# The output weights' four subtractions in the first pass of a decoder layer: from GpSimd to VectorE, in two pairs

## The chip, the cores and the metric

One core of a Trainium2 chip runs the kernel. The metric is the device time of one execution in microseconds (us). Engines are named as the profile does: PE is TensorE's matmul, PEld its weight load, DVE VectorE, ACT ScalarE, POOL GpSimd, SP SyncE, whose queue issues all the DMAs that the text speaks of.

## The reference, cut to what matters

One layer over 1024 positions of width 2048 in float32: one wide input projection, three mixers on its parts, an output projection, a residual and a layer norm.

```python
proj = jnp.einsum('bsd,de->bse', x, w_in[l])
...
y_att = forgetting_attention(...) * jax.nn.silu(g_att)
y_conv = short_conv_mixer(...) * jax.nn.silu(g_conv)
y_pool = multiscale_pool_mixer(...) * jax.nn.silu(g_pool)
y = jnp.concatenate([y_att, y_conv, y_pool], axis=-1)
y = jnp.einsum('bse,ed->bsd', y, w_out[l])
x = layer_norm(DEEPNORM_ALPHA * x + y, ln_g[l], ln_b[l])
```

Both projections are done by a fast block scheme (Strassen's, in a form with sums that share terms): each 2 x 2 block product takes seven products of blocks, and the blocks that go into them are sums and differences of the blocks of `x` and of the weights. For `w_out` these are the differences b22 - b12, b12 - b11, b22 - (b12 - b11) and b21 - (b22 - (b12 - b11)). Here the first pass makes them on the side and stores them in DRAM (`o_dram`), for the last stage of the kernel to load.

## The kernel before

**Products.** A float32 value goes into TensorE as two parts, high and low. `split` (L120) makes them: `L121` copies the source, rounded, on ScalarE (`hi`), and `L122` subtracts that from the source on VectorE (`lo`). `mm3` (L127) then runs three matmuls, `L128` high x high, `L129` high x low of `x`, `L130` low x high. So every operand of TensorE takes one `L121` and one `L122`, and the third matmul of a product is the first to need the result of `L122`. `operand` (L320) allocates both parts with the tag `h1`, name `wop`, in four buffers, which is two operands: the one in use and the next.

**The first pass** (`first_pass`, L529) goes over 28 pairs of weight columns, each a 2 x 2 of blocks of 128 x 1024. A pair's place in `order` is called turn n. Pairs 0 to 11 have turns of three products (steps `s2`, `s1`, `s3`), with the product `11` done before; pairs 12 to 27 have turns of four (`11`, `s2`, `s1`, `s3`). Up to turn 23 the two kinds alternate, three on even n, four on odd n; the last four turns are all of four. One product is 24 matmuls of 128x512, into a bank `aux` or `acc`. After `s2` VectorE adds the bank to `ca` (`L296`, to `u`); after `s1` it makes `cb` (`L304`); after `s3`, `ca` and `cb` (`L307`, `L308`), which are stored (`L309`, `L310`).

**What goes on beside a product** is written in `beside(p, name)` (L459), called after each. In the program's order: the next turn's pair is mixed (`Pair.mix`, L255, and `mix_last`, L268) at `s2` of a three-product turn or at `11` of a four-product one; the pair after that is loaded at `s1` (`load_place`, L252: blocks 0, 1, 3, 2, 512 KB each, tag `w1`, nine buffers, name `wb`). For the pairs of three products the mix is `L259` and `L260` on VectorE and `L261` on GpSimd; for those of four it is `L264` on GpSimd (`t`), and then `L265` and `L266` on VectorE. Each ends with `L270` on GpSimd, whose result is stored by `L273`. The scheduler draws mixes ahead of their written place: turn 11's, written at turn 10's `s2`, stands behind `L304` of turn 9 on VectorE.

**The output weights** are the class `OutBlocks` (L381). Sixteen of its blocks are done in turns 7 to 24, without 14 and 18 (`out_places`, L526). In such a turn n:

- at `s2`, `outs[n - 1].store()` (four stores of 256 KB, `L405`) and then `outs[n].load()` (four loads of 256 KB, `L392`, tiles `wo` of 128x512; three with the tag `wr`, which has four buffers, one with `wh`, which has three);
- at `s1`, `outs[n].mix()`: a fifth tile and four subtractions on GpSimd, `L397` to `L400`.

**What sets the order.** Each engine runs its instructions in one order, fixed when the program is built. A scheduler makes it out of the program's order and may move what is not held; `tc.keep_in_program_order` holds an instruction in its written place on its engine, as the stores and loads of `OutBlocks` are. The engines wait for each other by semaphores. The SP queue, too, is one order: a store in it that waits for its data holds every DMA behind it.

Of the kernel before, what the change touches and what calls it, by code (L numbers as in the profile page):

```python
# [36 lines left out]
ALU = mybir.AluOpType  # L37
# [36 lines left out]
def layer(ctx: ExitStack, tc: tile.TileContext, xt, x, wp, wf, b_f, conv_w, pool_w, pool_scale,  # L74
          w_out, ln_g, ln_b, out):
    nc = tc.nc
# [27 lines left out]
    def f4(name, tag):  # L104
        return tile_of([P, S], F32, name, tag)
# [5 lines left out]
    def half(name, tag):  # L111
        return tile_of([P, H], F32, name, tag)
# [128 lines left out]
    class Pair:  # L241
# [13 lines left out]
        def mix(self):  # L255
            r = self.raw
            if self.p < AHEAD:
                self.t1, self.t2, self.t3 = r[0], f4("t2", "w1"), r[1]
                nc.vector.tensor_tensor(self.t1, r[1], r[0], ALU.subtract)  # L259
                nc.vector.tensor_tensor(self.t2, r[3], self.t1, ALU.subtract)  # L260
                nc.gpsimd.tensor_tensor(self.t3, r[3], r[1], ALU.subtract)  # L261
            else:
                self.t1, self.t2, self.t3 = r[1], r[3], f4("t3", "w1")
                nc.gpsimd.tensor_tensor(self.t3, r[3], r[1], ALU.subtract)  # L264
                nc.vector.tensor_tensor(self.t1, r[1], r[0], ALU.subtract)  # L265
                nc.vector.tensor_tensor(self.t2, r[3], self.t1, ALU.subtract)  # L266

        def mix_last(self):  # L268
            r = self.raw
            nc.gpsimd.tensor_tensor(r[2], r[2], self.t2, ALU.subtract)  # L270
# [76 lines left out]
    def gate_sums(name, k0):  # L347

        acc = bank("aux")[: 2 * NH]
        for k in range(KH):  # L350
            w = fw[:, k0 + k].rearrange("p a b -> p (a b)")
            x = xs[name, k]
            nc.tensor.matmul(acc, w, x[:, 0], start=k == 0, stop=False)
            nc.tensor.matmul(acc, w, x[:, 1], start=False, stop=k == KH - 1)
        flat = half("gs", "wh")[: 2 * NH]
        nc.scalar.copy(flat, acc)
        return flat

    def turned_sums(flat):

        turned = bank("aux")[:, : 8 * NH].rearrange("p (a b) -> p a b", a=4)
        for st in range(4):
            nc.tensor.transpose(turned[:, st], flat[:, st * P : st * P + P], ident[: 2 * NH, : 2 * NH])
        return turned
# [3 lines left out]
    def load_s4(k):  # L368
        r21, r22, r11, r12 = (half("xr", "wr") for _ in range(4))
        for r, e, h in ((r21, k, 1), (r22, KH + k, 1), (r11, k, 0), (r12, KH + k, 0)):  # L370
            tc.keep_in_program_order(nc.sync.dma_start(r, xt[e, :, h * H : h * H + H]))
        s4_parts[k] = r21, r22, r11, r12

    def make_s4(k):
        r21, r22, r11, r12 = s4_parts.pop(k)
        nc.vector.tensor_tensor(r21, r21, r22, ALU.add)
        nc.vector.tensor_tensor(r21, r21, r11, ALU.subtract)
        nc.vector.tensor_tensor(r12, r12, r21, ALU.subtract)
        nc.sync.dma_start(s4_dram[k], r12)

    class OutBlocks:  # L381
# [5 lines left out]
        def load(self):  # L387
            i, k = self.i, self.k
            self.t = [half("wo", tag) for tag in ("wr", "wr", "wr", "wh")]
            for t, e, c in zip(self.t, (KH + k, KH + k, k, k), (0, 1, 0, 1)):  # L390
                src = w_out[e, :, i * S + c * H : i * S + c * H + H]
                tc.keep_in_program_order(nc.sync.dma_start(t, src))  # L392

        def mix(self):
            b11, b12, b21, b22 = self.t
            t3 = half("wo", "wh")
            nc.gpsimd.tensor_tensor(t3, b22, b12, ALU.subtract)  # L397
            nc.gpsimd.tensor_tensor(b12, b12, b11, ALU.subtract)
            nc.gpsimd.tensor_tensor(b22, b22, b12, ALU.subtract)
            nc.gpsimd.tensor_tensor(b21, b21, b22, ALU.subtract)  # L400
            self.t = b12, b22, t3, b21

        def store(self):
            for j, t in enumerate(self.t):
                tc.keep_in_program_order(nc.sync.dma_start(o_dram[self.i, j, self.k], t))  # L405
# [21 lines left out]
    def replace(name, tag, src):  # L427
        for k in range(KH):
            t = take(name, k, tag)
            r = half("xr", "wr")  # L430
            nc.sync.dma_start(r, src[k])
            split_tile(t, r)
# [30 lines left out]
    def load_place(n):  # L463
        order[n].load(0, 1, 3, 2)

    def beside(p, name):

        if name == "11" and p < AHEAD:
            if p == EARLY:
                load_place(0)  # L470
            if p == AHEAD - 2:
                load_place(1)
            if p == AHEAD - 1:
                order[0].mix()
                order[0].mix_last()
            return
        n = place[p]
        if name == ("s2" if p < AHEAD else "11") and n + 1 < N_PAIRS:
            order[n + 1].mix()
            order[n + 1].mix_last()  # L480
        if name == "s2" and n < N_PAIRS - 2:
            pairs[p].store_mixed()
            if n - 1 in outs:
                outs[n - 1].store()
            if n in outs:
                outs[n].load()
        if name in ("s2", "s3") and 3 <= n < 8:
            for k in s4_parts.copy():
                make_s4(k)
            if n < 7:  # L490
                load_s4(2 * n - 6 + (name == "s3"))
        if name == "s1":
            if n in outs:
                outs[n].mix()
            if n + 2 < N_PAIRS:
                load_place(n + 2)
            if n in gate_sums_at:
                env["sums"] = gate_sums(gate_sums_at[n], 0)
        if name == "s3":
            if n == 2:  # L500
                nc.vector.tensor_copy(fgt[:, :4], turned_sums(env["sums"]))
            if n == 3:
                nc.vector.tensor_tensor(fgt[:, 4:], fgt[:, :4], turned_sums(env["sums"]), ALU.subtract)
        if (n, name) == (N_PAIRS - 1, "11"):
            replace("12", "xa", xt[KH:, :, :H])
        if (n, name) == (N_PAIRS - 1, "s2"):
            for q in order[-2:]:
                q.store_mixed()
            replace("22", "xb", xt[KH:, :, H:])
        if (n, name) == (N_PAIRS - 1, "s1"):  # L510
            replace("s4", "xc", s4_dram)
            for q in (0, 1):
                t = half("c11", "wr")
                nc.sync.dma_start(t, a_dram[q, :, :H])
                banks_set.append(preset(t))

    def preset(block):

        acc = bank("acc")
        nc.scalar.copy(acc, block)  # L520
        return acc
# [4 lines left out]
    outs = {n: OutBlocks(m % 2, m // 2) for m, n in enumerate(out_places)}  # L526

    def first_pass():
        ahead_of = in_order()  # L529
        step = next(ahead_of)  # L530
        parts = operand(step[1]())
        while step:
            after_it = next(ahead_of, None)
            parts_after = None
            p, _, name, bank_of, follow = step
            if after_it and (p.p, name) != (AHEAD - 1, "11"):
                parts_after = operand(after_it[1]())
            multiply(parts, name, bank_of())
            follow()
            beside(p.p, name)  # L540
            if after_it and parts_after is None:
                parts_after = operand(after_it[1]())
            step, parts = after_it, parts_after
# [8 lines left out]
    def gate_logits(n):  # L552
# [12 lines left out]
    fgz, az, lf, before, t2, poly = (  # L565
        gate_tmp[:, i * NST * NH : (i + 1) * NST * NH].rearrange("p (a b) -> p a b", b=NH) for i in range(6))
# [244 lines left out]
    def pool_steps(g, u, gate):  # L811
# [43 lines left out]
        for slot, step in ((7, means), (9, split_pw), (13, split_z(0)), (14, split_z(1)), (16, mix(0)), (17, mix(1))):  # L855
            at(slot, step)
# [412 lines left out]
```

## Time and profile before

| | |
|---|---|
| time, median of 3 runs (lowest to highest) | 1660.64 us (1660.34 to 1664.97) |
| profiled execution: its own time, its span | 1661.48 us, 1659.4 us |
| PE busy in the span | 1561.2 us, 94% |
| DVE busy | 1116.7 us, 67% |
| ACT busy | 701.0 us, 42% |
| POOL busy | 517.4 us, 31% |
| DMA, mean | 205 GB/s |

The span is the profiled execution from its first to its last instruction; the execution's own time is longer by what lies around it. A busy share is a mean over the whole span, in which stages with different limits follow each other. Line numbers (L122) are those of the kernel before. A timeline's row gives the start, the duration, engine, line, operation and tile (out<-in), and in brackets how long the engine was idle before it and what ended that. A waits row gives the total idle time, the number of times and the longest.

### The profile page before, as it was taken

To read this page: it belongs to the slowest core of one execution; us is meant where nothing else is said; L and a number is where in the kernel's file an instruction comes from. 1 tells how busy PE (TensorE), PEld (TensorE's weight loads), DVE (VectorE), ACT (ScalarE), POOL (GpSimd) and SP (SyncE) were. 2 spreads that over 40 slices of the span, in tenths; PEclk is the share of its full clock that TensorE was granted. 3 is DMA by queue.
4 is the path that set the end of the run, shared out by engine and by line. 5 is a ranking of instruction groups with operands and counts; after the bars stand their busy time and mean duration, and the time that the engine had idled before them with its cause. 6 is when DMAs were issued, how large, how long until landed. Compare 5 with 4: busy or idle time off the path is not lost. (4 is left out here: it accounts for less than half of the span.)

```text
span 1659.4 us, 20213 instructions
## 1 busy us (share of the span) xinstructions
PE 1561.2 (94%) x6836; PEld 1258.9 (76%) x6836; DVE 1116.7 (67%) x1587; ACT 701.0 (42%) x1254; POOL 517.4 (31%) x381
## 2 busy tenths in 40 slices
PE   7999999999999989999999999989988999999985
PEld 6887777787787878788878777867766777788765
DVE  6754665676464556368686868677778884567777
ACT  4421211121111115457565657565666554434431
POOL 0132234666555541004141413343326231100005
PEclk9999999999999999999999999999999999999998
DMA  8755877887777775735545445445444446557552
GB/s 249 253 208 205 313 270 277 286 299 252 268 254 264 255 278 178 256 129 165 183 163 180 159 169 168 154 139 193 135 149 156 146 141 231 181 184 228 183 193 101
DMA packets 156807, 339.92 MB, mean 205 GB/s; under 512 B 17952, under 2 KB 27040, under 8 KB 156704
## 3 DMA queue, kind: packets, MB, share of 16 engines
q1 hardware_dynamic: 156704, 338.64, 60.2%
q8 instruction: 53, 0.87, 0.2%
q14 instruction: 50, 0.41, 0.1%
HBM read 247.28 MB, written 91.29 MB: 204 GB/s over the span
## 5 line engine op out<-in xcount | busy, mean ns | idle before, releaser
L122 DVE TENSOR_TENSOR wh<-wr,wh 128x512 fp32r<-128x512 f32 x272 | 203.2, 753 | 94.7 <-ACT wh L121 94.1
L121 ACT CAST wop<-wb 128x1024 fp32r<-128x1024 f32 x76 | 80.0, 1053 | 341.4 <-PE aux L129 173.1
L121 ACT CAST wh<-wr 128x512 fp32r<-128x512 f32 x272 | 166.4, 618 | 92.4 <-PE acc L130 27.8
L130 PE MATMUL aux<-xs,wop 128*128 128x512 f32 x448 | 178.4, 398 | 18.7 <-DVE wop L122 18.6
L130 PE MATMUL acc<-x,wh 128*128 128x512 f32 x448 | 177.6, 396 | 2.4 <-DVE wh L122 2.3
L128 PE MATMUL acc<-x,wh 128*128 128x512 f32 x448 | 178.4, 398 | 1.4 <-ACT wh L121 1.4
L128 PE MATMUL aux<-xs,wop 128*128 128x512 f32 x448 | 177.1, 395 | 0.0
L129 PE MATMUL aux<-xs,wop 128*128 128x512 f32 x448 | 176.6, 394 | 0.0
L129 PE MATMUL acc<-x,wh 128*128 128x512 f32 x448 | 176.2, 393 | 0.0
L122 DVE TENSOR_TENSOR wop<-wb,wop 128x1024 fp32r<-128x1024 f32 x76 | 120.6, 1587 | 41.6 <-ACT wop L121 41.5
L130 PEld LDWEIGHTS aux<-xs,wop 128*128 128x128 f32 x448 | 85.5, 191 | 42.2 <-DVE wop L122 23.9
L130 PEld LDWEIGHTS acc<-x,wh 128*128 128x128 f32 x448 | 84.6, 189 | 27.4 <-DVE wh L122 9.5
L128 PEld LDWEIGHTS acc<-x,wh 128*128 128x128 f32 x448 | 85.0, 190 | 20.5 <-ACT wh L121 5.1
L129 PEld LDWEIGHTS aux<-xs,wop 128*128 128x128 f32 x448 | 85.5, 191 | 18.3
L128 PEld LDWEIGHTS aux<-xs,wop 128*128 128x128 f32 x448 | 85.7, 191 | 17.8
L129 PEld LDWEIGHTS acc<-x,wh 128*128 128x128 f32 x448 | 85.1, 190 | 15.7
L130 PE MATMUL acc<-xs,wh 128*128 128x512 f32 x224 | 87.8, 392 | 3.4 <-DVE wh L122 3.4
L130 PE MATMUL acc<-xs,wop 128*128 128x512 f32 x224 | 87.7, 392 | 2.3 <-DVE wop L122 2.1
L704 POOL TENSOR_TENSOR m<-m,t 128x256 f32<-128x256 f32 (+1 forms) x64 | 69.9, 1092 | 63.2 <-ACT t L757 61.0
L128 PE MATMUL acc<-xs,wh 128*128 128x512 f32 x224 | 88.2, 394 | 0.0
L122 DVE TENSOR_TENSOR pt<-t,pt 128x512 fp32r<-128x512 f32 (+1 forms) x96 | 84.0, 888 | 6.3 <-ACT pt L121 6.1
L129 PE MATMUL acc<-xs,wh 128*128 128x512 f32 x224 | 87.4, 390 | 0.0
(269 smaller groups left out, 3733.1 us busy)
## 6 DMA issues: line engine op xcount, KB each, us to landing
wb<-wp SPq DMA_DIRECT2D x116, 512.0 KB, 5.7
wr<-wp SPq DMA_DIRECT2D x112, 256.0 KB, 2.8
wo<-w_out SPq DMA_DIRECT2D x64, 256.0 KB, 6.0
o_dram<-wo SPq DMA_DIRECT2D x64, 256.0 KB, 3.6
wr<-o_dram SPq DMA_DIRECT2D x64, 256.0 KB, 2.8
t_dram<-wb SPq DMA_DIRECT2D x28, 512.0 KB, 6.2
a_dram<-ca SPq DMA_DIRECT2D x28, 512.0 KB, 4.7
b_dram<-cb SPq DMA_DIRECT2D x28, 512.0 KB, 5.5
```

What stands on the lines that cost most here:

```text
L121: nc.scalar.copy(hi, src)
L122: nc.vector.tensor_tensor(lo, src, hi.bitcast(F32), ALU.subtract)
L128: nc.tensor.matmul(acc, wh, xh, start=start, stop=False, **more)
L129: nc.tensor.matmul(acc, wh, xl, start=False, stop=False, **more)
L130: nc.tensor.matmul(acc, wl, xh, start=False, stop=stop, **more)
L704: eng.tensor_tensor(kept[n][:, c0:], prev[:, c0:], t[n, j][:, c0:], op)
```

## The change

The four subtractions of `OutBlocks.mix` run on VectorE instead of GpSimd, through a helper (L395) that holds them in their written place. `mix`, at `s1`, keeps the first two. The last two move to a new `mix_last`, called at `s3`, after the third or fourth product of the turn. The lines behind move down: the stores from `L405` to `L411`. The arithmetic is the same.

```diff
--- before.py
+++ after.py
@@ -391,14 +391,20 @@
                 src = w_out[e, :, i * S + c * H : i * S + c * H + H]
                 tc.keep_in_program_order(nc.sync.dma_start(t, src))
 
+        def subtract(self, out, a, b):
+            tc.keep_in_program_order(nc.vector.tensor_tensor(out, a, b, ALU.subtract))
+
         def mix(self):
             b11, b12, b21, b22 = self.t
             t3 = half("wo", "wh")
-            nc.gpsimd.tensor_tensor(t3, b22, b12, ALU.subtract)
-            nc.gpsimd.tensor_tensor(b12, b12, b11, ALU.subtract)
-            nc.gpsimd.tensor_tensor(b22, b22, b12, ALU.subtract)
-            nc.gpsimd.tensor_tensor(b21, b21, b22, ALU.subtract)
+            self.subtract(t3, b22, b12)
+            self.subtract(b12, b12, b11)
             self.t = b12, b22, t3, b21
+
+        def mix_last(self):
+            t1, t2, _, t4 = self.t
+            self.subtract(t2, t2, t1)
+            self.subtract(t4, t4, t2)
 
         def store(self):
             for j, t in enumerate(self.t):
@@ -497,6 +503,8 @@
             if n in gate_sums_at:
                 env["sums"] = gate_sums(gate_sums_at[n], 0)
         if name == "s3":
+            if n in outs:
+                outs[n].mix_last()
             if n == 2:
                 nc.vector.tensor_copy(fgt[:, :4], turned_sums(env["sums"]))
             if n == 3:
```

The orders below show what that does. Numbers behind a name tell buffers apart; of the same tile they can differ by two between the kernels.

On VectorE, in turn 9 (four products), from the add after `s1` to the start of the mix of turn 12's pair (`L259`); `L265` and `L266` mix turn 11's. `cb` and `ca` are the adds from PSUM, `wop` the low halves, `wb` the pair's blocks, `wo` the output weights' blocks. Before:

```order
L304 TENSOR_TENSOR cb_2121<-acc_2096,u_335_2077 128x512
L265 TENSOR_TENSOR wb_2130<-wb_2130,wb_2128 128x1024
L122 TENSOR_TENSOR wop_2137<-t_331_2043,wop_2136 128x1024
L266 TENSOR_TENSOR wb_2132<-wb_2132,wb_2130 128x1024
L307 TENSOR_TENSOR ca_2041<-aux_2052,ca_2041 128x512
L308 TENSOR_TENSOR cb_2121<-acc_2096,ca_2041 128x512
L122 TENSOR_TENSOR wop_2169<-wb_1972,wop_2168 128x1024
L259 TENSOR_TENSOR wb_2255<-wb_2257,wb_2255 128x1024
```

With the change:

```order
L304 TENSOR_TENSOR cb_2121<-acc_2096,u_335_2077 128x512
L265 TENSOR_TENSOR wb_2128<-wb_2128,wb_2126 128x1024
L122 TENSOR_TENSOR wop_2135<-t_331_2043,wop_2134 128x1024
L395 TENSOR_TENSOR wo_2123<-wo_2087,wo_2085 128x512
L266 TENSOR_TENSOR wb_2130<-wb_2130,wb_2128 128x1024
L395 TENSOR_TENSOR wo_2085<-wo_2085,wo_2084 128x512
L307 TENSOR_TENSOR ca_2041<-aux_2052,ca_2041 128x512
L308 TENSOR_TENSOR cb_2121<-acc_2096,ca_2041 128x512
L395 TENSOR_TENSOR wo_2087<-wo_2087,wo_2085 128x512
L122 TENSOR_TENSOR wop_2169<-wb_1970,wop_2168 128x1024
L259 TENSOR_TENSOR wb_2253<-wb_2255,wb_2253 128x1024
L395 TENSOR_TENSOR wo_2086<-wo_2086,wo_2087 128x512
```

The four `L395` stand between the split of the second next product (`L122` from `t`) and the end of the turn: one ahead of `L266`, one ahead of the adds, one ahead of the next `L122` and one behind `L259`.

On VectorE, in turn 10 (three products), from the split ahead of `s3` to the one for turn 11's second product. Before:

```order
L122 TENSOR_TENSOR wop_2264<-wb_2128,wop_2263 128x1024
L260 TENSOR_TENSOR t_376_2326<-wb_2259,wb_2255 128x1024
L307 TENSOR_TENSOR ca_2172<-aux_2174,ca_2172 128x512
L308 TENSOR_TENSOR cb_2248<-acc_2223,ca_2172 128x512
L122 TENSOR_TENSOR wop_2296<-wb_2132,wop_2295 128x1024
L122 TENSOR_TENSOR wop_2332<-wb_2130,wop_2331 128x1024
```

With the change:

```order
L122 TENSOR_TENSOR wop_2262<-wb_2126,wop_2261 128x1024
L395 TENSOR_TENSOR wo_2250<-wo_2214,wo_2212 128x512
L260 TENSOR_TENSOR t_376_2326<-wb_2257,wb_2253 128x1024
L395 TENSOR_TENSOR wo_2212<-wo_2212,wo_2211 128x512
L307 TENSOR_TENSOR ca_2172<-aux_2174,ca_2172 128x512
L308 TENSOR_TENSOR cb_2248<-acc_2223,ca_2172 128x512
L395 TENSOR_TENSOR wo_2214<-wo_2214,wo_2212 128x512
L122 TENSOR_TENSOR wop_2296<-wb_2130,wop_2295 128x1024
L395 TENSOR_TENSOR wo_2213<-wo_2213,wo_2214 128x512
L122 TENSOR_TENSOR wop_2332<-wb_2128,wop_2331 128x1024
```

The first `L395` now stands ahead of `L260` and the second ahead of the adds; the last two have the adds and one `L122` ahead of them.

On SP's queue, from the stores of turn 8's block to the loads of turn 9's, with the loads of a pair between (blocks 0, 1, 3, 2 are `wb_2128`, `wb_2130`, `wb_2132`, `wb_2134` before, and 2126 to 2132 with the change). Before:

```order
L405 DMA o_dram<-wo_1929 128x512
L252 DMA wb_2130<-wp 128x1024
L405 DMA o_dram<-wo_1931 128x512
L405 DMA o_dram<-wo_1967 128x512
L405 DMA o_dram<-wo_1930 128x512
L392 DMA wo_2084<-w_out 128x512
L392 DMA wo_2085<-w_out 128x512
L252 DMA wb_2132<-wp 128x1024
L392 DMA wo_2086<-w_out 128x512
L252 DMA wb_2134<-wp 128x1024
```

With the change:

```order
L411 DMA o_dram<-wo_1929 128x512
L411 DMA o_dram<-wo_1931 128x512
L411 DMA o_dram<-wo_1967 128x512
L411 DMA o_dram<-wo_1930 128x512
L392 DMA wo_2084<-w_out 128x512
L392 DMA wo_2085<-w_out 128x512
L252 DMA wb_2128<-wp 128x1024
L252 DMA wb_2130<-wp 128x1024
L392 DMA wo_2086<-w_out 128x512
L252 DMA wb_2132<-wp 128x1024
```

The four stores now stand together, and the load of block 1 (`wb_2130` before, `wb_2128` now) comes behind them and two loads of `w_out`, where it stood behind the first store. TensorE's and ScalarE's orders are unchanged.

## Rows read from the trace of the kernel before

In the table by stretches an engine's entry is its busy time in us and, in brackets, its instructions; the clock is the mean granted clock of TensorE as a share of its full speed, DMA the busy share of the DMA engines.

**Rows 1.** Stretches; columns: stretch, length, PE, PEld, DVE, ACT, POOL, clock, DMA, GB/s.
```profile
241.00:612.00 371.00, 350.58 (x1503) 284.72 (x1502) 221.94 (x170) 71.16 (x73) 213.11 (x100) 0.98 0.76 265
445.00:465.00 20.00, 16.83 (x62) 13.32 (x61) 13.84 (x9) 2.10 (x2) 13.39 (x6) 0.83 0.83 290
530.00:550.00 20.00, 16.38 (x65) 13.02 (x64) 13.07 (x10) 3.16 (x3) 13.52 (x6) 0.91 0.82 291
605.00:625.00 20.00, 16.70 (x67) 13.34 (x66) 11.34 (x9) 3.64 (x4) 9.69 (x5) 0.91 0.69 250
```

**Rows 2.** Waits, 241 to 612 us: waiter <- releaser: total us, times, longest.
```profile
POOL t L264 <- DMA wb<-wp: 50.7, 6, 12.2
POOL wo L397 <- DMA wo<-w_out: 45.2, 8, 12.8
...
DVE wb L265 <- POOL t L264: 34.5, 10, 5.5
...
PE aux L130 <- DVE wop L122: 16.8, 9, 3.6
...
PE acc L130 <- DVE wop L122: 3.4, 3, 1.3
```

**Rows 3.** Timeline of PE, at two of its stalls.
```profile
449.46 0.39 PE L129 MATMUL aux<-xs,wop 128*128 128x512 f32 x1
453.02 0.80 PE L130 MATMUL aux<-xs,wop 128*128 128x512 f32 x1 [3.17 <-DVE wop L122]
...
609.22 0.73 PE L130 MATMUL aux<-xs,wop 128*128 128x512 f32 x1 [3.30 <-DVE wop L122]
```

**Rows 4.** Timeline of DVE, end of turn 16 to start of turn 18.
```profile
427.67 0.69 DVE L307 TENSOR_TENSOR ca<-aux,ca 128x512 f32<-128x512 f32 x1 [0.46 <-PE aux L130]
...
429.00 1.56 DVE L122 TENSOR_TENSOR wop<-wb,wop 128x1024 fp32r<-128x1024 f32 x1
...
443.99 0.69 DVE L304 TENSOR_TENSOR cb<-acc,u 128x512 f32<-128x512 f32 x1 [3.31 <-PE acc L130]
449.54 1.23 DVE L265 TENSOR_TENSOR wb<-wb,wb 128x1024 f32<-128x1024 f32 x1 [4.86 <-POOL t L264]
450.68 2.28 DVE L122 TENSOR_TENSOR wop<-t,wop 128x1024 fp32r<-128x1024 f32 x1
452.89 2.29 DVE L266 TENSOR_TENSOR wb<-wb,wb 128x1024 f32<-128x1024 f32 x1
...
456.42 3.29 DVE L122 TENSOR_TENSOR wop<-wb,wop 128x1024 fp32r<-128x1024 f32 x1
```

**Rows 5.** Timeline of POOL, same turns, and the last of the sixteen.
```profile
426.05 3.43 POOL L261 TENSOR_TENSOR wb<-wb,wb 128x1024 f32<-128x1024 f32 x1 [10.14 <-DMA wo<-w_out]
...
437.79 1.29 POOL L400 TENSOR_TENSOR wo<-wo,wo 128x512 f32<-128x512 f32 x1
447.11 2.40 POOL L264 TENSOR_TENSOR t<-wb,wb 128x1024 f32<-128x1024 f32 x1 [8.03 <-DMA wb<-wp]
449.71 2.18 POOL L397 TENSOR_TENSOR wo<-wo,wo 128x512 f32<-128x512 f32 x1 [0.20 <-DMA wo<-w_out]
...
456.27 2.36 POOL L270 TENSOR_TENSOR wb<-wb,wb 128x1024 f32<-128x1024 f32 x1
...
600.99 1.28 POOL L397 TENSOR_TENSOR wo<-wo,wo 128x512 f32<-128x512 f32 x1 [12.82 <-DMA wo<-w_out]
```

**Rows 6.** Timeline of SP's queue, same turns: start, duration, line, transfer.
```profile
437.74 1.69 SPq L405 DMA_DIRECT2D o_dram<-wo  x3
...
440.67 0.46 SPq L252 DMA_DIRECT2D wb<-wp  x1
```

**Rows 7.** Timeline of DVE, before the output weights begin.
```profile
225.72 0.68 DVE L377 TENSOR_TENSOR xr<-xr,xr 128x512 f32<-128x512 f32 x1
226.32 1.22 DVE L260 TENSOR_TENSOR t<-wb,wb 128x1024 f32<-128x1024 f32 x1
```

**Rows 8.** DVE by form, 241-612 us: xcount | busy, mean | idle.
```profile
L122 DVE TENSOR_TENSOR wop<-wb,wop 128x1024 fp32r<-128x1024 f32 x46 | 81.8, 1778 | 21.3 <-ACT wop L121 21.3
```

## The prediction

> **What bounds the kernel now.** I read four views, in this order: the table by stretches, the waits, the timelines of one stalled turn, and the issue queue. The change touches only the stretch from 241 to 612 us, in which the sixteen blocks of the output weights are mixed. TensorE is busy for 350.6 of its 371 us [rows 1], so what can be gained there is what TensorE loses. The waits give it: 16.8 us before `aux` products and 3.4 us before `acc` products, 20.2 us in 12 stalls, all ended by VectorE's `wop L122`, the low half of the next operand [rows 2]. Beside that the clock is lowered after the three longest stalls: mean granted clock 0.83, 0.91 and 0.91 over 20 us each [rows 1], so the matmuls after them run partly at the lower of its two levels (1.2 for 2.4 GHz). That is (0.17 + 0.09 + 0.09) x 20 = 7.0 us. Together 27 us; as a second bound, 1503 matmuls [rows 1] at 5.44 us per 24 (three products lie between the adds at 427.67 and 443.99 [rows 4]) take 341 us, 30 us less than the stretch. More than 30 us cannot come of this change.
>
> Turn 17 to 18 shows why `L122` is late. TensorE stops at 449.46 + 0.39 and goes on at 453.02 [rows 3]. The `L122` that it waits for ran from 450.68 for 2.28 us, behind `L265` at 449.54, which had waited 4.86 us for GpSimd's `L264` [rows 4]. `L264` ran from 447.11 to 449.51, having waited for a load of weights [rows 5]: the load of block 3, issued at 440.67, after the issue queue had been held by stores of the output weights until 437.74 + 1.69 [rows 6]. Those stores wait for GpSimd's last subtractions (`L400`, 437.79 + 1.29 [rows 5]). So GpSimd's output weights do harm twice: they delay loads through the queue, and they lengthen VectorE's subtractions. A 128x1024 subtraction of VectorE takes 1.22 us alone [rows 7], 2.28 beside `L397` at 449.71, 3.29 beside `L270` at 456.27, and GpSimd's half-size one 1.29 alone and 2.18 beside VectorE [rows 4, 5]: the one runs while the other stands. The 46 splits of raw blocks took 81.8 us [rows 8] where 46 x 1.22 is 56.1. The adds from PSUM keep their 0.69 us [rows 4].
>
> **The change, part by part.** *Removed from GpSimd:* 64 subtractions, each of which holds VectorE's up for about 1.1 us (2.28 - 1.22) when they meet. GpSimd keeps `L261`, `L264` and `L270` and has cover to spare.
>
> *Added to VectorE:* 64 subtractions of 128x512 from SBUF. The row nearest to them is `L377`: 0.68 us, the next starting 0.60 later [rows 7]. 64 x 0.60 = 38 us, in a stretch where VectorE is busy 222 of 371 us [rows 1]; the 26 us of lengthening in the 46 splits alone pay most of it back. Lower bound of the price of one: 0.60; upper bound: 0.60 + 2.40 where it meets an `L264` or `L270` first [rows 5]. I take 0.60, and one such meeting per turn.
>
> *The chain after `L264`.* Let F be its end. Now `L122` ends 3.4 us after F (452.96 - 449.51), and the one for the following product 10.2 us after F (456.42 + 3.29) [rows 4]. With the change, in the order shown above: `L265` 1.14, `L122` 1.14, so 2.3 us after F. Then a subtraction 0.60, `L266` 1.14, a subtraction 0.60, the two adds 1.3, a subtraction 0.60, `L122` 1.14: 7.7 us after F, or 8.7 where `L270` stands in between.
>
> *F itself.* In a three-product turn the last subtraction now stands behind the adds `L307`, `L308` and one `L122`. At turn 16: `L307` at 427.67, `L122` from 429.00 [rows 4], with 0.60 ahead of it and 0.60 behind it: ready at 431.5, or 433.9 if `L270` holds VectorE for 2.40. GpSimd was ready at 439.08. The queue is freed 5.2 to 7.6 us earlier, and with it the load of block 3, for which I keep its 6.4 us (440.67 to 447.11); block 1, which `L264` needs as well, now stands ahead of it behind the four stores and costs the queue 0.5 more. F becomes 442.4 to 444.8 instead of 449.5. The next turn wants its low half at 449.85 (453.02 - 3.17) [rows 3]; after F `L265` and `L122` take 2.3 us, so they end by 447.1. The stall of 3.17 us goes, and the half speed after it. The following `L122` comes by 444.8 + 8.7 = 453.5 and is wanted a product later, at 449.85 + 5.44 = 455.3. The other stalls before the last three turns have the same chain or only the lengthening, and go too.
>
> *The new hold.* The first subtraction now waits on VectorE for the block's load, with everything behind it: `L266` or `L260`, the adds, the next `L122`. GpSimd waited 45.2 us for those loads, 8 times [rows 2]. In a three-product turn the latest landing that can be read at turn 16 is 426.05 [rows 5]. From there: subtraction, `L260`, subtraction, two adds, subtraction, `L122` = 0.6 + 1.14 + 0.6 + 1.3 + 0.6 + 1.14 = 5.4 us, 431.4, or 433.8 with one meeting with `L270`; wanted a product after the adds, at about 427.67 + 5.44 = 433.1. It just fits. At the last of the sixteen turns the load landed at 600.99 [rows 5]; two subtractions, `L265`, an add, `L266` and `L122` then take 0.6 + 0.6 + 1.14 + 0.69 + 1.14 + 1.14 = 5.3 us, 606.3; TensorE stopped at 605.92 (609.22 - 3.30) [rows 3]: 0.4 left of 3.30. For such remnants, and meetings that I did not follow, I leave 2 us.
>
> *Sum:* 20.2 + 7.0 - 2 = 25 us. The profiled execution took 1661.48 us (span 1659.4, 2.1 around it), 0.8 above the median of 1660.64, so 1636.5 against its own time and 1635.6 against the median: I say 1636. Where these stalls go, the next thing late is the block's load in the three-product turns.
>
> The row on `L397` beside `L122` says that a subtraction moved off GpSimd gives VectorE 1.1 us and costs it 0.6 [rows 4, 5, 7]. The Trainium skill (Perfetto Trace Analysis, Optimizing Scalar/DVE Operations) warns that the two engines share a port, so that offloading between them might not help; by it the stretch would stay as it is, 1660.6 us. That is the fourth case below.
>
> **The rivals.** *The load stays late (partial).* The lengthening goes, but block 3 is not earlier, since other entries hold the queue. For: in the changed order block 1 moves behind all four stores, just ahead of it. Against: the stores are ready 5 us earlier. F stays, `L122` comes 1.1 us sooner: of stalls such as 3.17 us some 2 us stay, in the three longest with their half speed. About 10 to 17 us are gained: 1644 to 1651.
>
> *VectorE held by the block's load (slower).* Place: the first subtraction in the six three-product turns with a block and the last two turns. `L265` shows the mechanism: it waits 34.5 us in all for `L264` [rows 2], and `L122` stands behind it. The margin at turn 16 is 433.1 - 431.4 = 1.7 us without the meeting, none with it; if the loads land 4 us later than now, each of the eight turns stalls by 2 to 4 us, 16 to 32 us with half speed after some, against some 15 us that are still gained: about 1670. It decides from landings some 3 us later. Against: these loads wait for the stores before them, and those go out sooner. The Trainium skill (TensorE: Matmul & The Clock Gate, Architectural detail) calls VectorE's queue a strict FIFO; by that rule, too, every wait for a block's load is passed on to the split behind it.
>
> *Nothing measurable.* New holds and meetings eat what the lengthening gave, 1660.6 us; by the rows above 64 x 0.6 added stands against 64 x 1.1 at most, so it asks that few meetings are removed. That the change does not do what it says is excluded by the order: the subtractions stand there, and TensorE's and ScalarE's orders are unchanged.
>
> **How the numbers follow.** What a measurement can tell from no change is about 0.3%, 5 us. Forecast (1630 to 1643) 0.62; load stays late 0.18; nothing measurable 0.10; slower 0.10. The first two are faster by over 0.3%: 0.80. The range reaches from all 30 us down to the partial case: 1629 to 1652, which leaves out the last two cases.
>
> **What would show it.** Right: no TensorE wait over 1 us between 241 and the end of the first pass, granted clock 0.98 or more there, `L265` and `L122` near 1.22 us, the last store of a three-product turn some 5 us sooner after `L307`, and `L264` ended 4 us before the next turn. Wrong: the subtraction `L395` idle for a load of `w_out` with a TensorE stall right behind it, or a first pass that ends where it did.

## The result, and the profile after

The change took 1637.75 us (median of 4 runs, 1636.92 to 1640.37) against 1660.72 before: 23.0 us less, a ratio of 0.9852 with a 95% interval of 0.9832 to 0.9871. Forecast were 1636 and a range of 1629 to 1652. Measured a second time beside other kernels it took 1640.95 against 1663.52, ratio 0.9867 (0.9844 to 0.9889). The time came out nearly as the sum had it; several parts of the sum did not, as the rest of this text shows.

To compare traces I take the stretch from the start of turn 6's `L307` (the last add before the first subtraction) to that of turn 27's (the end of the pass). The table by stretches, before (columns as in [rows 1]):

```profile
228.06:673.80 445.74, 425.32 (x1829) 344.92 (x1828) 266.17 (x225) 101.14 (x116) 224.12 (x105) 0.98 0.75 261
```

and after:

```profile
224.20:650.92 426.72, 418.81 (x1829) 340.65 (x1828) 279.62 (x290) 101.11 (x116) 104.75 (x42) 1.00 0.77 272
```

The stretch is 445.74 - 426.72 = 19.0 us shorter, for the same 1829 matmuls. Of these, 425.32 - 418.81 = 6.5 us is TensorE's own busy time: the granted clock went from 0.98 to 1.00, so no matmul ran at the lower level any more. The other 12.5 us are idle time of TensorE. The waits of the change, from 241 to 595 us, columns as in [rows 2]:

```profile
POOL t L264 <- DMA wb<-wp: 121.1, 9, 15.1
...
DVE wb L265 <- POOL t L264: 23.6, 7, 4.6
...
DVE wo L395 <- DMA wo<-w_out: 13.9, 6, 4.4
...
PE aux L130 <- DVE wop L122: 5.2, 7, 1.3
...
PE acc L130 <- DVE wop L122: 2.5, 5, 0.6
```

TensorE's waits fell from 20.2 us [rows 2] to 7.7. None is over 1.4 us; before, three were over 3. (The sign of being right that the prediction named was none over 1 us; two are, 1.35 and 1.18.) VectorE now waits 13.9 us, six times, for blocks of `w_out`: the new hold. GpSimd waits 121.1 us for weights in front of `L264`, where it had waited 50.7 [rows 2]: it is ready long before them.

VectorE's groups in the same stretch (xcount | busy us, mean ns | idle before):

```profile
L122 DVE TENSOR_TENSOR wop<-wb,wop 128x1024 fp32r<-128x1024 f32 x46 | 68.0, 1477 | 9.3 <-ACT wop L121 9.3
L395 DVE TENSOR_TENSOR wo<-wo,wo 128x512 f32<-128x512 f32 x64 | 66.2, 1034 | 17.6 <-DMA wo<-w_out 13.9 <-DMA wb<-wp 3.5
...
L266 DVE TENSOR_TENSOR wb<-wb,wb 128x1024 f32<-128x1024 f32 x11 | 13.4, 1219 | 0.0
```

The last of these before, 241 to 612 us:

```profile
L266 DVE TENSOR_TENSOR wb<-wb,wb 128x1024 f32<-128x1024 f32 x11 | 24.1, 2195 | 0.0
```

`L266` is down from 2.2 us in the mean to 1.22, but the splits of raw blocks only from 1.78 [rows 8] to 1.48, and a new subtraction takes 1.03 us in the mean, where one alone takes 0.68 (priced at 0.60, the time until the next one starts).

The same turn as before the change, 17 to 18. VectorE:

```profile
417.72 0.69 DVE L395 TENSOR_TENSOR wo<-wo,wo 128x512 f32<-128x512 f32 x1 [2.38 <-DMA wo<-w_out]
...
420.06 0.68 DVE L307 TENSOR_TENSOR ca<-aux,ca 128x512 f32<-128x512 f32 x1
...
424.01 0.68 DVE L395 TENSOR_TENSOR wo<-wo,wo 128x512 f32<-128x512 f32 x1
...
439.06 1.23 DVE L265 TENSOR_TENSOR wb<-wb,wb 128x1024 f32<-128x1024 f32 x1 [3.35 <-POOL t L264]
440.21 1.22 DVE L122 TENSOR_TENSOR wop<-t,wop 128x1024 fp32r<-128x1024 f32 x1
...
445.01 1.56 DVE L395 TENSOR_TENSOR wo<-wo,wo 128x512 f32<-128x512 f32 x1
446.50 1.21 DVE L122 TENSOR_TENSOR wop<-wb,wop 128x1024 fp32r<-128x1024 f32 x1
```

GpSimd:

```profile
436.63 2.40 POOL L264 TENSOR_TENSOR t<-wb,wb 128x1024 f32<-128x1024 f32 x1 [14.23 <-DMA wb<-wp]
443.24 2.78 POOL L270 TENSOR_TENSOR wb<-wb,wb 128x1024 f32<-128x1024 f32 x1 [4.21 <-DVE wb L266]
```

The issue queue:

```profile
422.67 4.42 SPq L411 DMA_DIRECT2D o_dram<-wo  x4
...
428.54 0.85 SPq L252 DMA_DIRECT2D wb<-wp  x2
```

TensorE:

```profile
440.49 0.39 PE L129 MATMUL aux<-xs,wop 128*128 128x512 f32 x1
441.48 0.50 PE L130 MATMUL aux<-xs,wop 128*128 128x512 f32 x1 [0.61 <-DVE wop L122]
...
447.76 0.50 PE L130 MATMUL acc<-xs,wop 128*128 128x512 f32 x1 [0.55 <-DVE wop L122]
```

The stall of 3.17 us [rows 3] became one of 0.61 and one of 0.55, and both kinds come again in other four-product turns. The first is the old chain: `L264` ends at 439.03, `L122` at 441.43, and its result was wanted at 440.87. The second is new: a subtraction that ran beside `L270` for 1.56 us, with the next `L122` behind it.

`L307` is itself late here. These are the last matmuls of the product that it adds, before and after:

```profile
427.25 0.39 PE L130 MATMUL aux<-xs,wop 128*128 128x512 f32 x1
```

```profile
418.27 0.39 PE L130 MATMUL aux<-xs,wop 128*128 128x512 f32 x1
```

Before, `L307` (427.67) followed the end of the product at once; now (420.06) it comes 1.40 us after it, because VectorE had stood 2.38 us for a load ahead of it. In turns 10 and 12 it is 1.3 us late in the same way, and was 0.04 before. Measured from the end of the product, `L264` ends 20.37 us later, where it was 21.87 before: 1.50 us sooner. The `L122` behind it ends 2.40 us after `L264`, where it was 3.45: 1.05 sooner, as nothing there is lengthened any more. Together that is what this stall lost (3.17 - 0.61). By the same measure `L264` came 3.1 us sooner at turn 21, whose stall of 3.62 us went, but 2.5 later at turn 13, where there is now a stall of 1.35; why it is later there I did not trace.

A third kind stands after turns 22, 23 and 24. VectorE and TensorE after turn 24:

```profile
581.38 2.51 DVE L395 TENSOR_TENSOR wo<-wo,wo 128x512 f32<-128x512 f32 x2 [3.82 <-DMA wo<-w_out]
```

```profile
587.95 0.50 PE L130 MATMUL aux<-xs,wop 128*128 128x512 f32 x1 [1.18 <-DVE wop L122]
```

Here subtractions that waited for a load stand, with no gap behind them, ahead of the split. Of the 7.7 us of stalls, 2.6 stand behind a late `L264` (four stalls), 2.5 behind a subtraction beside `L270` (five), and 2.7 behind such a wait for a load (three).

A subtraction at 445.01 beside an `L270` that runs from 443.24 to 446.02 ends at 446.57, 0.55 after it: it looks as if it did its work when GpSimd had ended. The Trainium skill (SBUF — State Buffer, section "SBUF: two separate sides") says just that: a VectorE operation with two SBUF inputs and a GpSimd operation that reads SBUF lock the ports that they share, and the later one blocks until the other is done. The trace agrees: what is left of the subtraction after `L270`, 0.55 us, is nearly the 0.68 of one alone.

### The profile page after: what moved, and what is told of

It reads as the page before. It is cut to its first block, busy times and chain, and to the rows that moved or that the text cites. A ratio compares the mean times of both kernels' runs of the same rounds, so it can differ in the third digit from the quotient of the medians.

```text
span 1635.2 us, 20207 instructions
## 1 busy us (share of the span) xinstructions
PE 1553.2 (95%) x6836; PEld 1254.1 (77%) x6836; DVE 1132.4 (69%) x1651; ACT 702.0 (43%) x1254; POOL 400.0 (24%) x317
## 5 line engine op out<-in xcount | busy, mean ns | idle before, releaser
L122 DVE TENSOR_TENSOR wh<-wr,wh 128x512 fp32r<-128x512 f32 x272 | 204.0, 755 | 97.7 <-ACT wh L121 97.3
L130 PE MATMUL aux<-xs,wop 128*128 128x512 f32 x448 | 175.5, 392 | 5.4 <-DVE wop L122 5.2
L128 PE MATMUL aux<-xs,wop 128*128 128x512 f32 x448 | 174.6, 390 | 0.0
L129 PE MATMUL aux<-xs,wop 128*128 128x512 f32 x448 | 174.4, 389 | 0.0
L122 DVE TENSOR_TENSOR wop<-wb,wop 128x1024 fp32r<-128x1024 f32 x76 | 107.0, 1408 | 28.2 <-ACT wop L121 28.1
L130 PEld LDWEIGHTS aux<-xs,wop 128*128 128x128 f32 x448 | 84.1, 188 | 27.3 <-DVE wop L122 9.6
L129 PEld LDWEIGHTS aux<-xs,wop 128*128 128x128 f32 x448 | 84.1, 188 | 17.6
L128 PEld LDWEIGHTS aux<-xs,wop 128*128 128x128 f32 x448 | 84.1, 188 | 17.4
L130 PE MATMUL acc<-xs,wop 128*128 128x512 f32 x224 | 88.0, 393 | 2.7 <-DVE wop L122 2.5
L122 DVE TENSOR_TENSOR pt<-t,pt 128x512 fp32r<-128x512 f32 (+1 forms) x96 | 84.5, 894 | 6.5 <-ACT pt L121 6.3
L128 PE MATMUL acc<-xs,wop 128*128 128x512 f32 x224 | 87.2, 389 | 0.0
```

Source lines behind the costliest of these rows:

```text
L122: nc.vector.tensor_tensor(lo, src, hi.bitcast(F32), ALU.subtract)
L128: nc.tensor.matmul(acc, wh, xh, start=start, stop=False, **more)
L129: nc.tensor.matmul(acc, wh, xl, start=False, stop=False, **more)
L130: nc.tensor.matmul(acc, wl, xh, start=False, stop=stop, **more)
```

## The experiments

The traces of before, of the change (twice) and of eleven more kernels are set side by side here. "Stretch" is the one defined above, "stalls" TensorE's idle time in it that a result of VectorE ended; both are from one profiled execution. That one is not always near the median: x5's took 1653.85 us, x2's 1654.55 and x12_all_late's 1631.60. Only the change has two traces; their stretches differ by 1.0 us. The ratio is to the kernel before in the same set of runs.

| kernel | subtractions on | median us | ratio (95%) | stretch us | stalls us |
|---|---|---|---|---|---|
| before | GpSimd | 1660.72 | 1 | 445.74 | 20.2 |
| the change | VectorE | 1637.75 | 0.9852 (0.9832 to 0.9871) | 426.72 | 7.7 |
| c_after (again) | VectorE | 1640.95 | 0.9867 (0.9844 to 0.9889) | 427.68 | 8.0 |
| x1_none | none | 1628.22 | 0.9788 (0.9765 to 0.9810) | 415.17 | 0.2 |
| x2_gps_split | GpSimd | 1664.22 | 0.9993 (0.9971 to 1.0016) | 448.49 | 21.7 |
| x3_dve_free | VectorE | 1656.87 | 0.9964 (0.9947 to 0.9982) | 443.88 | 20.5 |
| x5_scratch | VectorE | 1643.15 | 0.9895 (0.9870 to 0.9921) | 432.81 | 12.8 |
| x6_pair_dve | VectorE | 1639.20 | 0.9859 (0.9836 to 0.9882) | 425.83 | 9.7 |
| x9_late | VectorE | 1642.69 | 0.9878 (0.9857 to 0.9899) | 423.43 | 6.5 |
| x11_s3 | VectorE | 1631.87 | 0.9805 (0.9785 to 0.9825) | 415.11 | 0 |
| x12_all_late | VectorE | 1637.43 | 0.9844 (0.9815 to 0.9874) | 419.00 | 2.9 |
| x12_gps | GpSimd | 1632.40 | 0.9809 (0.9782 to 0.9835) | 417.01 | 1.7 |
| x13_before_loads | GpSimd | 1651.51 | 0.9920 (0.9893 to 0.9948) | 425.38 | 7.8 |
| x14_after_loads | VectorE | 1657.39 | 0.9962 (0.9938 to 0.9985) | 431.29 | 11.5 |

The theory I set out with (A): the change gains because GpSimd's subtractions no longer lengthen VectorE's and because the stores of the output weights are ready earlier. The main rival (B): the queue alone, block 3's load behind stores that wait.

**x1_none**: how much is left.

```diff
-            t3 = half("wo", "wh")
-            self.subtract(t3, b22, b12)
-            self.subtract(b12, b12, b11)
-            self.t = b12, b22, t3, b21
+            self.t = b12, b22, b11, b21
...
-            self.subtract(t2, t2, t1)
-            self.subtract(t4, t4, t2)
+            pass
```

> The 64 subtractions of the output weights are left out; the blocks are loaded and stored as they come. Theory A (the change gains by ending GpSimd's meetings with VectorE and by earlier stores, and what is left is the load of block 3 being late): the stalls of 0.55 us behind a subtraction on VectorE go, the others stay, 1632 to 1636 us. Rival C (what is left is VectorE held by the subtractions' waits for their loads): all 7.7 us of stalls of the first pass go, 1628 to 1631 us. If the subtractions on VectorE cost nothing at all: 1637 to 1639 us.

All stalls but 0.2 us went, as rival C had it: the stretch is 11.6 us shorter than with the change. So the 64 subtractions on VectorE were not free. This run alone doesn't tell what they cost, VectorE's time or the stores that wait for them.

**x5_scratch**: the meetings alone.

```diff
             tc.keep_in_program_order(nc.vector.tensor_tensor(out, a, b, ALU.subtract))
+            tc.keep_in_program_order(nc.gpsimd.tensor_tensor(idle, idle, idle, ALU.subtract))
```

(`idle` is a tile of its own; the lines that make and fill it are left out.)

> The change as it is, and beside each subtraction on VectorE one of the same size on GpSimd that reads and writes a tile of its own, on which nothing waits. Theory A (meetings of the two engines cost): VectorE's splits are lengthened again, their mean goes from 1.48 towards 1.75 us, and stalls of 5 to 15 us come back, 1642 to 1652 us. Rival B (the gain is the earlier stores alone, the lengthening fell into VectorE's idle time): the splits are longer and the time stays, 1636 to 1640 us.

VectorE's groups, 241 to 600 us (`L397` is the subtraction of the output weights here):

```profile
L122 DVE TENSOR_TENSOR wop<-wb,wop 128x1024 fp32r<-128x1024 f32 x45 | 80.6, 1791 | 7.1 <-ACT wop L121 7.1
L397 DVE TENSOR_TENSOR wo<-wo,wo 128x512 f32<-128x512 f32 x64 | 79.2, 1238 | 19.7 <-DMA wo<-w_out 13.7 <-DMA wb<-wp 3.0 <-DMA xr<-xt 2.8
```

The splits are as long as before the change (1.79 against 1.78 us [rows 8]), and the stretch grows by 6.1 us over the change's. In 12 of the 13 stalls the split that TensorE waits for (2.06 us) or the subtraction right ahead of it (1.57) is lengthened, and GpSimd's `L264` is not late by the added work: it waits for its loads (60.2 us). So lengthening costs something here, in this execution a third of what the change gained in the stretch: theory A, at the low end of its range. By the medians alone it could hardly be told from the change: the intervals of the two ratios overlap.

**x9_late and x6_pair_dve**: two tries at what was left. x9 moves the last two subtractions to just ahead of the stores:

```diff
-            if n in outs:
-                outs[n].mix_last()
...
             if n - 1 in outs:
+                outs[n - 1].mix_last()
                 outs[n - 1].store()
```

> The last two subtractions, still on VectorE, come one or two products later (at s2 of the next turn, just ahead of the stores), so that the stores of a three-product turn are ready some 6 us later, as they were before; the scheduler then puts the loads of blocks 1, 3 and 2 ahead of three of the four stores. Theory A (what is left is block 3 behind the stores in the queue): L264 ends 3 us or more earlier in a four-product turn and the stalls before aux products go, 1630 to 1635 us. Rival C (what matters is when the output weights land, since VectorE is held for them): their loads now stand behind late stores, subtractions hold the splits, 1641 to 1655 us.

x6 takes GpSimd out of the pass (the same edit at `L261` and `L264`):

```diff
-            nc.gpsimd.tensor_tensor(r[2], r[2], self.t2, ALU.subtract)
+            nc.vector.tensor_tensor(r[2], r[2], self.t2, ALU.subtract)
```

> The change, and the three kinds of subtraction of the pairs that GpSimd still does (L261, L264, L270) also on VectorE, so that GpSimd is idle in the first pass. Theory A: no subtraction on VectorE is lengthened, splits at 1.22 us, L264 takes 1.2 us less on the chain; VectorE gets 56 x 1.14 = 64 us over the pass, of which the end of lengthening gives some 30 back; 1631 to 1636 us. Rival D (VectorE's queue becomes the bound, each late load held on it): new stalls of 1 to 2 us in most turns, 1642 to 1660 us.

Neither moved the time clearly from the change's: x9 lies in rival C's range, x6 between its two. x9's stretch is 3.3 us shorter, but subtractions that stand ahead of `L260` or `L265` now wait longer for their loads:

```profile
DVE wo L395 <- DMA wo<-w_out: 23.9, 8, 5.2
...
PE aux L130 <- DVE wop L122: 6.5, 7, 2.1
```

x6 reached what theory A asked for, no lengthening at all:

```profile
L122 DVE TENSOR_TENSOR wop<-wb,wop 128x1024 fp32r<-128x1024 f32 x46 | 56.0, 1217 | 11.8 <-ACT wop L121 11.8
L395 DVE TENSOR_TENSOR wo<-wo,wo 128x512 f32<-128x512 f32 x64 | 43.8, 684 | 16.0 <-DMA wo<-w_out 10.6 <-issue 4.9
```

and TensorE still stalls for 9.7 us, seven times. But six of these stalls are of its own making, as rival D had it: three stand behind `L264`, which now waits 6.1 to 6.8 us for weights on VectorE, and three behind the `L261` that was added ahead of a split. So x6 doesn't show what the end of the lengthening alone would give.

**x11_s3, x12_all_late, x12_gps**: late subtractions, and the engine by itself. x11 is x9 with the first two subtractions after `s3`:

```diff
-            if n in outs:
-                outs[n].mix()
             if n + 2 < N_PAIRS:
...
         if name == "s3":
+            if n in outs:
+                outs[n].mix()
```

x12 calls `mix` and `mix_last` together at the next turn's `s2`, and x12_gps is x12 with `nc.gpsimd` in `subtract`. In all three the scheduler puts the loads of blocks 1 and 3 ahead of all or most of the stores.

> The change once more, beside the other kernels of this set: 1634 to 1641 us by every theory; in its trace the splits and L395 as long as in the first profile (1.47 and 1.03 us).

> All four subtractions on VectorE, the first two after s3 instead of s1 and the last two at s2 of the next turn; the scheduler then puts blocks 1 and 3 ahead of the stores, and no subtraction stands ahead of L260, L266 or the adds of its own turn. Theory A (what the change left are two waits: block 3 behind the stores in the queue, and splits behind a subtraction that waits for its load): stalls of TensorE in the first pass under 2 us instead of 7.7, 1625 to 1632 us. Rival E (what is left is VectorE's added work itself, 64 times 0.7 to 1 us): 1635 to 1641 us.

> All four subtractions on VectorE at s2 of the next turn, just ahead of the stores, with blocks 1, 3 and 2 ahead of the stores in the queue. Theory A: stalls under 3 us, 1625 to 1633 us. Rival E: 1635 to 1641 us. Four subtractions in a row stand ahead of L265 or L304 here; should that be what holds VectorE, stalls before the product after s1 come instead, 1635 to 1645 us.

> The same places and nearly the same queue, but all four subtractions on GpSimd, as before the change. Rival B (the queue alone: late stores ahead of block 3): the time falls as with VectorE, 1627 to 1636 us. Theory A (meetings of the engines cost by themselves): the splits stay at 1.7 us or more, and stalls of 8 to 15 us remain, 1640 to 1652 us.

c_after came out as expected in time. In its trace the subtractions are as long as in the first (1.04 us, 241 to 597 us), but the splits of raw blocks take 1.29 us in the mean, not 1.48: how much they are lengthened differs from one execution to the next.

x11's stretch by the table by stretches:

```profile
226.49:641.60 415.11, 415.11 (x1832) 342.20 (x1831) 261.85 (x289) 101.10 (x116) 103.43 (x43) 1.00 0.83 279
```

TensorE is busy for all of its 415.11 us. Its `L395` never wait for a load, and in most turns `L264` no longer waits for weights, but for VectorE to let a buffer go:

```profile
L395 DVE TENSOR_TENSOR wo<-wo,wo 128x512 f32<-128x512 f32 x64 | 53.8, 841 | 0.2
```

```profile
POOL t L264 <- DVE wop L122: 89.1, 8, 13.0
```

x12_gps was the surprise. GpSimd subtracts, VectorE's splits are nearly as long as before the change (1.65 against 1.78 us [rows 8]) and `L260` is longer, though `L266` is not lengthened any more (241 to 600 us):

```profile
L122 DVE TENSOR_TENSOR wop<-wb,wop 128x1024 fp32r<-128x1024 f32 x48 | 79.0, 1646 | 27.6 <-ACT wop L121 27.6
...
L260 DVE TENSOR_TENSOR t<-wb,wb 128x1024 f32<-128x1024 f32 x7 | 17.7, 2532 | 0.2
...
L266 DVE TENSOR_TENSOR wb<-wb,wb 128x1024 f32<-128x1024 f32 x11 | 13.4, 1214 | 0.0
```

and TensorE waits once in the whole stretch:

```profile
PE aux L130 <- DVE wop L122: 1.7, 1, 1.7
```

Theory A wanted 8 to 15 us of stalls here. At turn 21 `L264` ends 17.1 us after the product's end, where it was 22.3 before, so that the `L122` behind it is in time though it ends 4.6 us after `L264` (3.5 before). (x12's own stalls are nearly all before `acc` products, 2.7 of 2.9 us, as the four subtractions in a row let one expect.) Rival B holds: with the loads ahead of the stores and the subtractions this late it does not matter which engine subtracts (417.0 us on GpSimd, 419.0 on VectorE).

**x13_before_loads, x14_after_loads**: the queue alone. In the kernel before (x13) and in the change (x14) one call is moved:

```diff
             pairs[p].store_mixed()
+            load_place(n + 2)
             if n - 1 in outs:
...
-            if n + 2 < N_PAIRS:
-                load_place(n + 2)
```

> The kernel before with one call moved: the next but one pair's loads are written at s2, ahead of the stores of the output weights, instead of s1; the four subtractions stay on GpSimd where they were. Theory B (the queue: block 3 behind stores that wait for GpSimd): stalls of 20.2 us fall below 5, 1630 to 1640 us. Theory A (GpSimd's meetings with VectorE cost by themselves): half of the stalls stay, 1644 to 1655 us.

> The change with the same one call moved. Theory B: with block 3 ahead of the stores it no longer matters which engine subtracts, so within 5 us of the same kernel with GpSimd, 1630 to 1638 us, stalls below 5 us. Theory A: faster than that one by 8 us or more. Rival C (subtractions that wait for their loads hold VectorE, and these loads now come later): 1640 to 1650 us.

The moved call acts in the early turns too, and there it harms: turn 6's `L307` starts at 235.14 in x13, 7.1 us later than before. The median, 1651.51, lies in theory A's range and not in B's. For the question of the queue I read the stretch: 20.4 us shorter than before, with every subtraction where it was on GpSimd. Of these, 12 matmuls that now run ahead of the stretch (1817 in it for 1829) are 2.7 us, so some 17.7 compare with the change's 19.0. The lengthening did not stay as it was either: `L266`, 2.19 us before, takes 1.26 here, so the moved loads changed the meetings of the two engines too. What is left of TensorE's waits in x13:

```profile
PE aux L130 <- DVE wop L122: 4.9, 6, 2.3
PE aux L128 <- DVE u L296: 2.9, 2, 1.9
```

Rival B had asked for less than 5 us of stalls: the old kind is at 4.9, and 2.9 are a new one. x14, whose median of 1657.39 lies above every range named, is worse than x13 in the stretch, by 5.9 us: the loads of `w_out` come later, and on VectorE the subtractions' waits for them (26.4 us, 9 times) stand ahead of splits. On GpSimd, x13's longer waits for the same loads (70.8 us) hold up little.

**x2_gps_split and x3_dve_free**: the parts of the change. x2 has the change's places on GpSimd, x3 has VectorE without the holding:

```diff
-            tc.keep_in_program_order(nc.vector.tensor_tensor(out, a, b, ALU.subtract))
+            tc.keep_in_program_order(nc.gpsimd.tensor_tensor(out, a, b, ALU.subtract))
```

```diff
-            tc.keep_in_program_order(nc.vector.tensor_tensor(out, a, b, ALU.subtract))
+            nc.vector.tensor_tensor(out, a, b, ALU.subtract)
```

> The change's written places (two at s1, two at s3, all held) with the subtractions on GpSimd: the engine alone undone. All theories that let the engine or the earlier stores count: as before the change, 1655 to 1665 us. Were it the places alone, 1636 to 1642 us.

> The change without holding the subtractions in their written place; the scheduler orders them. On VectorE the only difference in the turns of a stall is that the third subtraction stands one instruction earlier, ahead of one of the two adds. Theory F (it is the engine and the time at which the stores become ready that count): as the change, 1636 to 1645 us. Rival G (the holding decides): 1648 to 1665 us.

The places alone give nothing. But the engine alone gives hardly more, 0.4% for the change's 1.5%, and what I expected of x3 was wrong: I had compared the two orders in turns 9 to 11 only. In later turns the scheduler puts a subtraction ahead of a split, or all four ahead of the adds. VectorE in turn 16 of x3:

```profile
423.51 2.43 DVE L395 TENSOR_TENSOR wo<-wo,wo 128x512 f32<-128x512 f32 x1 [3.49 <-DMA wo<-w_out]
425.87 1.21 DVE L122 TENSOR_TENSOR wop<-wb,wop 128x1024 fp32r<-128x1024 f32 x1
```

The split had nothing to wait for but the subtraction, which waited for its load and then for GpSimd. TensorE:

```profile
424.80 0.39 PE L129 MATMUL acc<-x,wop 128*128 128x512 f32 x1
427.13 0.50 PE L130 MATMUL acc<-x,wop 128*128 128x512 f32 x1 [1.95 <-DVE wop L122]
```

This is the rival "VectorE held by the block's load", complete; in the change the held order keeps that `L122` ahead of the subtraction. But two such stalls are 2.6 of the 20.5 us. The larger part, 12.9 us in ten stalls, stands behind a subtraction that met `L270` on GpSimd. VectorE, GpSimd and TensorE in turn 17 of x3:

```profile
454.63 2.29 DVE L395 TENSOR_TENSOR wo<-wo,wo 128x512 f32<-128x512 f32 x1
456.84 1.21 DVE L122 TENSOR_TENSOR wop<-wb,wop 128x1024 fp32r<-128x1024 f32 x1
```

```profile
453.64 2.73 POOL L270 TENSOR_TENSOR wb<-wb,wb 128x1024 f32<-128x1024 f32 x1 [3.13 <-DVE wb L266]
```

```profile
458.11 0.50 PE L130 MATMUL acc<-xs,wop 128*128 128x512 f32 x1 [2.03 <-DVE wop L122]
```

These subtractions take 2.28 to 2.77 us. In the change the third one stands behind both adds, so that most of `L270` is over when it starts, and takes 1.56. In the other four stalls of x3, 5.1 us, two to four subtractions in a row, the first after a wait for its load, stand ahead of `L265`.

## Why the prediction was right, and where it was not

**The bound.** Right: I had put 30 us as the most that could come, and x1 and x11, which have next to no stalls left, are 30.6 us shorter in the stretch.

**The clock.** 7.0 us forecast, 6.5 measured. With the three longest stalls the lower level of the clock went as a whole.

**The stalls.** 18.2 us of 20.2 were to go; 12.5 went. The term that was mis-sized is the step "*F itself*", the end of `L264`. I had it at 14.7 to 17.1 us after the three-product turn's `L307` (442.4 to 444.8 against 427.67); it came 439.03 - 420.06 = 19.0 after, where it had been 21.8 before; and as `L307` was itself 1.4 us late, against TensorE's product it came 1.5 us earlier, for 4.7 to 7.1 forecast. Piece by piece at that turn: the subtractions were done in time, 4.6 us after `L307` (424.01 + 0.68; forecast 3.8 to 6.2). But the four stores, now together, took the queue 4.42 us and left it free 2.4 us after the last subtraction, at 427.09, where it had been 0.35 (439.43 against 439.08). That is 7.0 us after `L307` instead of 11.8, so 4.7 earlier (forecast 5.2 to 7.6, the low end just missed). And the loads of blocks 1 and 3 now leave side by side, at 428.54 to 429.39, and `L264` started 7.2 to 8.1 us later, not the 6.4 that block 3 took when block 1 had gone ahead. Moving block 1 behind the stores was noted and priced at 0.5 us of issue alone; the transfer's own share was left out. What came behind F was right: `L122` 2.4 us after it (forecast 2.3), the following one 8.7 us after it where `L270` stands between (446.50 + 1.21 - 439.03; forecast 8.7).

**The new hold.** Seen, but sized too low. The prediction took 426.05 [rows 5] for the latest landing at turn 16, but that row is `L261`, which reads the pair's blocks. By the trace's landing times the fourth load of `w_out`, which the first subtraction needs, landed at 427.97 before the change; 5.4 us from there is 433.4, with no margin to the 433.1 at which the split was wanted. In the change these loads landed sooner against the product, as the prediction had argued. Still, the wait of 2.38 us at turn 16 held up `L307` and with it the last two subtractions and the stores, and three other waits ended in 2.7 us of stalls, where all remnants together had been given 2. That it costs more when the order changes, x3 and x14 showed.

**GpSimd's lengthening.** In the sum it had the smaller share (1.1 us from `L265` and `L122`, against 4.7 to 7.1 from F), and it came as forecast: 1.05 us at turn 17, beside the 1.50 that F gave. How the 19.0 us divide between the two over the whole stretch, no run separates. What the runs bound is each by itself: x5 prices the lengthening at some 6 us where the chain is tight, x3 has 12.9 us of stalls behind lengthened subtractions, and x12_gps, which kept much of it, lost the stalls, as `L264` came early enough. So what decides is when block 3 lands, and what stands ahead of a split on VectorE, with the time that GpSimd adds to it. Nor did the lengthening end: GpSimd kept three operations per pair, and the splits of raw blocks were still at 1.48 us (1.29 in c_after), the new subtractions at 1.03, where one alone takes 0.68.

**The total.** The stretch gave 19.0 us, less than the 25 that I forecast for it, while the medians differ by 23.0 and 22.6. The rest lies elsewhere: the profiled execution of the change was 3.9 us ahead already at turn 6's `L307`, where no subtraction had run. That start moves from one execution to the next with the same work in it (220.96 to 228.06 us in the kernels of the table, without x6, x13 and x14, which alter earlier turns). So the agreement of the medians with the forecast, within 2 us, is partly luck. The cause of those last 4 us stays open.

**The warning** of the Trainium skill (Perfetto Trace Analysis, Optimizing Scalar/DVE Operations), that moving work between these two engines might not help, agrees with x12 against x12_gps (419.0 and 417.0 us). For this change it would have been a wrong forecast, since the move also altered when the stores were ready.

**A version beyond both.** x11_s3 took 1631.87 us, 1.9% less than before and some 9 us less than the change in the same set. It leaves no stall in the stretch, and is there level with the kernel that does not subtract at all.

## What to carry to other kernels

An operation that nobody waits for can still set the time, if its store stands in a queue ahead of a load that matters: ask first what its store holds, then which engine runs it. On an engine that works in order, the place of an added operation that waits for a load, or that another engine can hold up, is worth more than its duration alone: it belongs behind the next operand that TensorE wants, late enough that its load has landed. And a moved transfer has two prices, the issue and the share of the transfers beside it.

## What the runs showed of the hardware that I had not expected

That VectorE's subtractions could be lengthened by a third and more (splits of 1.65 us, `L260` at 2.53, for 1.22 alone) with next to no effect on the time (x12_gps), while half-size ones of 2.28 to 2.77 us for 0.68 alone, right ahead of a split, cost up to 2.3 us of stall each (x3). That four stores together held the queue for 4.42 us, where three had taken 1.69 [rows 6]. And that, at the one turn followed, two loads of 512 KB issued together kept the operation behind them waiting for 7.2 to 8.1 us after their issue, where the second of them, issued with the first already under way, had taken 6.4.
